# Scoring the far old keys of sample attention on VectorE, with later ScalarE parts and turns by chunk, in a one-core decoder step

## The chip, the core and the metric

The kernel runs on one core of a Trainium2 chip. The core has TensorE (PE; its weight loads are listed apart as PEld), VectorE (DVE), ScalarE (ACT), GpSimd (POOL) and SyncE (SP), which here issues nearly all DMA transfers. The metric is the device time of one execution in microseconds. The kernel before takes 2691.39 us, the median of three runs between 2690.68 and 2692.33.

## The reference

One layer of a decoder is computed for a prompt of 256 tokens and for 8 sequences of 8 new tokens each, which have 2048 cached keys and values. All is float32, and so are the weights. Cut to what matters here:

```python
x += 0.5 * swiglu(rmsnorm(x), w_ffa_in, w_ffa_out)
x += token_mixer(rmsnorm(x))
x += 0.5 * swiglu(rmsnorm(x), w_ffb_in, w_ffb_out)

# token_mixer
qk_pre, mv, mo, mif, aq, ak, av, gm, ga = split_cols(h @ w_in)
hm, state = mlstm(silu(conv(qk_pre)), mv, gates(mif), state)
hm = hm * rsqrt(mean(hm * hm) + EPS);  hm = sigmoid(mo) * hm * m_norm
ha = dilated_attention(aq * 128 ** -0.5, [cached k, ak], [cached v, av])
merged = sigmoid(gm) * (hm @ w_pm) + sigmoid(ga) * (ha @ w_pa)
return merged @ w_out

# mlstm, per head: the read-out
h = num / maximum(abs(den), exp(-m))

# dilated attention, 8 heads of 128 channels: three patterns (window, stride)
PATTERNS = ((128, 1), (512, 4), (2048, 16))
for (w, d), bias in zip(PATTERNS, biases):
    s = einsum('bthe,btjhe->bhtj', q, k_all[:, qi - d * arange(w // d + 1)]) + bias
    m = max(s); p = exp(s - m); den = sum(p); num = p @ v      # one part
# the parts are joined by their maxima and sums, as one softmax over all of them
```

For a sample token the first two patterns reach 512 positions back ("near" keys), the third up to 2048 at every 16th position. Of the old positions beyond 512 each of the 8 new tokens of a sequence has its own 96 ("far" keys): 16m + t for token t. So the 8 tokens together have 768 far keys, of which each uses every eighth.

## The kernel before, in words

**The stream of weights.** All weights are read from HBM once, in chunks of 512 KB (`raw`, five buffers, loaded by SP's queue): four blocks of 128 rows by 256 output columns. Every chunk is split into a high half (`hi`, a cast on ScalarE, L198) and a low half (`lo`, the difference on VectorE, L199), and the tokens likewise (`xh` and `xl`, `bh` and `bl`). The 320 tokens (256 of the prompt, 64 new ones) are the columns of each matmul. A chunk takes TensorE 24 matmuls into a foreground PSUM tile (`fg`): two column blocks, four row blocks, and three products xh·hi, xl·hi and xh·lo. `run_job` works off the chunks of one output tile; at each chunk it first runs the entries that `later` has put off, then splits the chunk two ahead (`split_upto(ci + HLB)`, three buffers of each half), then steps the background work, then issues the 24 matmuls, and then asks for the next loads. Each engine works in the order in which the program is written.

**The order of the jobs.** The first SwiGLU has chunks 0 to 271, the mixer's input projections 272 to 448 (attention's q, k and v first, then mLSTM's, then the gates gm and ga), `w_pm` 449 to 464 (eight jobs of two chunks), `w_pa` 465 to 480, `w_out` 32 chunks, then the second SwiGLU. `w_pm` multiplies the mLSTM heads' result (`hr`), `w_pa` the attention's (`ar`).

**Background work.** Prompt attention, sample attention and mLSTM are Python generators that wait in lists: `every` is stepped at each chunk, `even` and `odd` at every second one, and `slow`, which holds sample attention, at 8 of 15 chunks (`pace`). A step issues its instructions between the split and the chunk's matmuls, into background PSUM tiles (`bg`, four buffers). Whatever of it is left when the first job of `w_pa` opens is run off there by `pa_open`, and behind it come the four loads of `ar` and their split into `bh` and `bl`.

**Sample attention.** There are 16 units: two groups of four heads by eight sequences. A unit's scores are 128 rows (4 heads x a quarter of the keys x 8 tokens): 16 matmuls take 320 old keys each (`kd` against the queries `qbd`), of which 128 near and 192 far ones, and 4 small ones the new keys (`kS` against `qS`). A softmax over 328 columns follows (`ss`), three transposes turn the probabilities (`pts`), and 44 matmuls multiply them with the values (`vt`, `vn`). The result of a unit is scaled on its way out of PSUM into `osb`; after each fourth unit `combine` transposes four of them, copies them to `hsS`, and writes them to DRAM (`ha_d`), from which the split of `ar` reads.

Of the kernel before, what the change touches and what calls it, by code (L numbers as in the profile page):

```python
# [32 lines left out]
SCOLS = 328  # L33
# [23 lines left out]
def _consts():  # L57
# [4 lines left out]
    for i in range(4):  # L62
        for t in range(8):
            mk[:, i, t, 0:128] = _logmult(512 + t - 128 * i - p)
            mk[:, i, t, 128 + t:320:8] = 0.0
            if i == 0:
                mk[:, i, t, 320:328] = _logmult(t - np.arange(8))
# [19 lines left out]
    c["mix"] = np.concatenate([bd, sel, sels, parts, qmask, cm], axis=1)  # L87
# [9 lines left out]
M_BD, M_SEL, M_SELS, M_PT, M_QM, M_CM = 0, 32, 64, 128, 132, 388  # L97
MIXW = 836


def decoder_kernel(tc, I, O, K):
    nc = tc.nc
    V, S, G, T = nc.vector, nc.scalar, nc.gpsimd, nc.tensor
# [10 lines left out]

    def mm(out, a, b, start=True, stop=True, **kw):
        T.matmul(out, a, b, start=start, stop=stop, **kw)  # L116
# [11 lines left out]
    later_q = []  # L128
# [4 lines left out]
    def run_later(force=False):  # L133
        rest = []
        for e in later_q:
# [23 lines left out]
    RAWB, HLB, KDB = 5, 3, 6  # L159
# [84 lines left out]
    def run_job(job):  # L244
# [4 lines left out]
        for n, (ci, k0, nk) in enumerate(cs):  # L249
            run_later()  # L250
# [5 lines left out]
            if ci > 3:  # L256
                split_upto(ci + HLB)
            if tick[0] % 2 == 0:
# [52 lines left out]
    def tr(out, in_):  # L311
        k = in_.shape[0]
        T.transpose(out, in_, ident[:k, :k])  # L313
# [9 lines left out]
    vs_d = dp.tile([NS, 1024], F32, name="vs_d")  # L323
    qs_d = [dp.tile([128, 256], F32, name=f"qs_d{i}") for i in range(2)]
# [161 lines left out]
    def aq_evac(ps, p):  # L486
# [3 lines left out]
        QT[p] = q  # L490

# [96 lines left out]
    def sample_attention():  # L588
        bdm = M["mix"][:, M_BD:M_BD + 32]
        pts = mxt([128, 4, 152], "pts", 1, "pts")  # L590
        sm = mxt([128, 7, 32], "sm", 1, "sm")
        vn = mxt([128, 512], "vn", 1, "vn")
        G.memset(vn, 0.0)
        G.memset(pts, 0.0)
        G.memset(sm, 0.0)
        G.memset(sm[:, 4], 1.0)
        KD = {}

        def load_k(n):
            if n < 64:  # L600
                KD[n] = mxt([128, 4, 320], "kd", KDB, "kd")
                dma(KD[n], I["old_k"][n].rearrange("p (j c) -> p j c", j=4))

        VT = {}
# [24 lines left out]
        for n in range(KDB):  # L629
            load_k(n)  # L630
# [4 lines left out]
        for _ in range(3):  # L635
            yield
# [21 lines left out]

        def soft(u, sp):
# [3 lines left out]
            V.tensor_reduce(sm[:, 0, 0:1], s, op=OP.max, axis=AX.X)  # L663
# [4 lines left out]
            S.activation(s, s, AF.Exp, bias=sm[:, 3, 0:1], accum_out=sm[:, 4, 0:1])  # L668
            return s

        def keys(u, h):
            later(lambda: load_k(4 * u + KDB + h), 1)
# [6 lines left out]
        def pv(u, ob):  # L679
            cs = [(128, 0, 8 * i, i // 2, i % 2) for i in range(4)]  # L680
            cs += [(128, 1, 8 * i, 2 + i // 2, i % 2) for i in range(4)]
            cs += [(128, 2, 16 * i, 4, i) for i in range(2)]
            cs += [(128, 3, 0, 5, None)]
# [929 lines left out]
```

## Time and profile before

| | |
|---|---|
| time, median of 3 runs | 2691.39 us (2690.68 to 2692.33) |
| the profiled execution's own time | 2691.68 us |
| its span in the profile | 2689.9 us |
| mean granted TensorE clock | 0.998 of full speed |
| busy: PE, PEld | 99%, 98% |
| busy: DVE, ACT, POOL | 53%, 39%, 6% |
| DMA | 554.5 MB, 206 GB/s over the span |
| one chunk's matmuls on TensorE | 24 of 320 columns |

Busy shares are averages over the whole span. The first and the second SwiGLU are about two thirds of it and look alike throughout; attention and mLSTM lie between about 890 and 1660 us. There the lists of background work add matmuls to TensorE, small operations to VectorE and ScalarE, and the cached keys, values and states to the DMA queue. In the profile's rows an fp32 matmul leaves two records, so counts of them are twice those of the program. Durations of single matmuls overlap, since they are pipelined; the distance from start to start is what one costs.

### The profile page before, as it was taken

Reading aid. Unit: us, or ns where it says so; the run is one execution under the profiler, and the core shown is the slowest. Engines: PE = TensorE matmul, PEld = TensorE weight load, DVE = VectorE, ACT = ScalarE, POOL = GpSimd, SP = SyncE. Lnnn points to the kernel's source line nnn. Section 1 sums busy time; section 2 is a strip of 40 time slices with the busy share of each in tenths; the row PEclk is TensorE's granted clock in tenths of the full one; section 3 lists DMA queues with packets and bytes.
Section 4 is the critical chain, followed back from the end, with each engine's and each line's share of the span. In section 5 each row is a group of like instructions: output and inputs, shape, how many; then the busy total and the mean of one; then the engine's idle time right before and its main releaser. Section 6 shows DMA issues by size and latency. Waiting matters only on the chain.

```text
span 2689.9 us, 49844 instructions
## 1 busy us (share of the span) xinstructions
PE 2674.0 (99%) x21176; PEld 2635.3 (98%) x21176; DVE 1429.3 (53%) x1703; ACT 1051.0 (39%) x1289; POOL 156.7 (6%) x190
## 2 busy tenths in 40 slices
PE   9999999999999999999999999999999999999998
PEld 9999999999999999999999999999999999999998
DVE  6444444444446565666655555655444454444445
ACT  5333333333335433444443334444333333333334
POOL 0100000000000000111111100000000000000000
PEclk9999999999999999999999999999999999999999
DMA  6554545445546678798999986655454544445443
GB/s 236 164 164 165 159 163 164 158 160 162 165 157 199 227 257 287 272 366 314 344 349 330 330 285 218 204 184 163 157 165 161 161 164 161 161 153 171 163 152 131
DMA packets 186779, 554.51 MB, mean 206 GB/s; under 512 B 26288, under 2 KB 53432, under 8 KB 186556
## 3 DMA queue, kind: packets, MB, share of 16 engines
q1 hardware_dynamic: 185836, 550.02, 60.5%
q8 instruction: 165, 2.70, 0.4%
q10 hardware_dynamic: 720, 1.31, 0.1%
q14 instruction: 58, 0.48, 0.1%
HBM read 520.05 MB, written 31.20 MB: 205 GB/s over the span
## 4 chain that ended last, share of the span: by engine, by line
PE 98%; DVE 1%; DMA 1%; ACT 0%; issue 0%; SPq 0%; DVEq 0%; ACTq 0%
PE fg L116 92%; PE bg L116 5%; PE bg L313 1%; DMA raw<-in_w_ffa_in_dram 0%; DVE lo L199 0%; DMA x<-in_x_t_dram 0%; ACT hi L198 0%; DVE x L1506 0%; SPq L113 0%; DMA raw<-in_w_in_dram 0%; DVE ss L364 0%; DVE rows L783 0%; ACT sq L363 0%; DVE rows L792 0%; ACT lg L1494 0%
## 5 line engine op out<-in xcount | busy, mean ns | idle before, releaser
L199 DVE TENSOR_TENSOR lo<-raw,hi 128x1024 fp32r<-128x1024 f32 (+1 forms) x780 | 958.6, 1235 | 924.7 <-ACT hi L198 902.0
L116 PE MATMUL fg<-xh,hi 128*128 128x320 f32 x4232 | 1270.9, 301 | 1.5 <-ACT hi L1421 1.5
L116 PE MATMUL fg<-xh,lo 128*128 128x320 f32 x4232 | 1261.5, 299 | 0.5 <-DVE lo L199 0.5
L116 PE MATMUL fg<-xl,hi 128*128 128x320 f32 x4232 | 1261.3, 299 | 0.0
L198 ACT CAST hi<-raw 128x1024 fp32r<-128x1024 f32 (+1 forms) x780 | 797.2, 1027 | 1059.7 <-PE fg L116 926.0
L116 PEld LDWEIGHTS fg<-xh,hi 128*128 128x128 f32 x4232 | 798.5, 189 | 8.3 <-issue 4.9
L116 PEld LDWEIGHTS fg<-xh,lo 128*128 128x128 f32 x4232 | 798.6, 189 | 1.0 <-DVE lo L199 1.0
L116 PEld LDWEIGHTS fg<-xl,hi 128*128 128x128 f32 x4232 | 798.7, 189 | 0.7
L116 PE MATMUL fg<-hh,hi 128*128 128x320 f32 x1408 | 421.2, 299 | 0.0
L116 PE MATMUL fg<-hl,hi 128*128 128x320 f32 x1408 | 421.0, 299 | 0.0
L116 PE MATMUL fg<-hh,lo 128*128 128x320 f32 x1408 | 421.0, 299 | 0.0
L116 PEld LDWEIGHTS fg<-hh,hi 128*128 128x128 f32 x1408 | 266.1, 189 | 0.1
L116 PEld LDWEIGHTS fg<-hl,hi 128*128 128x128 f32 x1408 | 266.1, 189 | 0.1
L116 PEld LDWEIGHTS fg<-hh,lo 128*128 128x128 f32 x1408 | 266.1, 189 | 0.0
L424 POOL TENSOR_TENSOR gt<-gt,rstd 128x640 f32<-128x640 f32 x44 | 68.0, 1546 | 1775.6 <-ACT gt L423 1775.6
L116 PE MATMUL fg<-bh,hi 128*128 128x320 f32 x512 | 153.3, 299 | 0.0
L116 PE MATMUL fg<-bl,hi 128*128 128x320 f32 x512 | 153.1, 299 | 0.0
L116 PE MATMUL fg<-bh,lo 128*128 128x320 f32 x512 | 153.1, 299 | 0.0
L116 PEld LDWEIGHTS fg<-bh,hi 128*128 128x128 f32 x512 | 96.8, 189 | 0.2 <-issue 0.2
L116 PEld LDWEIGHTS fg<-bl,hi 128*128 128x128 f32 x512 | 96.8, 189 | 0.0
L116 PEld LDWEIGHTS fg<-bh,lo 128*128 128x128 f32 x512 | 96.8, 189 | 0.0
L412 ACT CAST hh<-hf 128x640 fp32r<-128x640 f32 x44 | 34.5, 785 | 144.3 <-DVE hf L430 144.3
(266 smaller groups left out, 1157.4 us busy)
## 6 DMA issues: line engine op xcount, KB each, us to landing
raw<-in_w_in_dram SPq DMA_DIRECT2D x176, 512.0 KB
raw<-in_w_ffb_in_dram SPq DMA_DIRECT2D x176, 512.0 KB
raw<-in_w_ffa_in_dram SPq DMA_DIRECT2D x172, 512.0 KB
raw<-in_w_ffa_out_dram SPq DMA_DIRECT2D x80, 512.0 KB
kd<-in_old_k_dram SPq DMA_DIRECT2D x64, 640.0 KB
vt<-in_old_v_dram SPq DMA_DIRECT2D x80, 512.0 KB
raw<-in_w_ffb_out_dram SPq DMA_DIRECT2D x80, 512.0 KB
raw<-in_w_out_dram SPq DMA_DIRECT2D x32, 512.0 KB
```

What stands on the lines that cost most here:

```text
L116: T.matmul(out, a, b, start=start, stop=stop, **kw)
L198: S.copy(hi[:, :nk], t[:, :nk])
L199: V.tensor_tensor(lo[:, :nk], t[:, :nk], hi[:, :nk].bitcast(F32), op=OP.subtract)
L313: T.transpose(out, in_, ident[:k, :k])
L412: S.copy(h, xe)
L424: G.tensor_tensor(gt, gt, bcast(rstd, 2), op=OP.mult)
```

## The change

**Far keys on VectorE.** The 16 score matmuls of a unit take 128 columns of near keys (`nk`) in place of 320. The far keys come as rows: `fk` tiles of 128 keys by four heads of 128 channels, six blocks a unit in three tiles. VectorE multiplies a block with the queries `qr` (the row of token t at each key of token t, read 16 times over from a copy of the queries in DRAM, `qt_d`, that each aq job now writes through two transposes). Four of the six blocks are summed by row on ScalarE (16 Copy activations with an accumulator, 128 x 128 each), two by a reduction on VectorE. The far keys have their own maximum, exponentials and sums: two numbers a head (`fr`) are brought into the near keys' score tile by four matmuls of two columns with a selection matrix `tsel`, and take part in its softmax as one more column. The far probabilities (`pf`) multiply the far values in 24 matmuls into columns of their own, and a `join` adds the two results with weights `rw`. The near probabilities need two transposes in place of three. Near keys come in 32 loads and far keys in 48, of 512 KB each; before there were 64 of 640 KB.

**Who is stepped when.** `pace` is gone. Sample attention is stepped with `even` at every second chunk, mLSTM stays on the other ones, and odd units have one step more. A new list, `fill`, holds the far keys' work; at each chunk it is stepped for as long as VectorE "has room": `Metered` counts 0.16 us and 0.00104 us an element for every VectorE instruction that goes through it, and compares with 3.2 us a chunk plus an allowance for the background matmuls.

**ScalarE's parts later.** A queue `soon` is run right behind the split, so that what is put there is issued behind the high half of the chunk that comes two later: the exponentials, the copies of the probabilities, the scaled copy and the join, the far row sums, and the mLSTM norm's logarithm and exponential.

**mLSTM's read-out.** |den| is taken by ScalarE. The heads are no longer divided by max(|den|, exp(-m)): its square, times EPS, is added under the root of the norm instead, which comes to the same result.

```diff
+class Metered:
+    def __init__(self, engine):
+        self.engine, self.load, self.debt = engine, 0.0, 0.0
+
+    def __getattr__(self, name):
+        fn = getattr(self.engine, name)
+
+        def call(*a, **k):
+            n = math.prod((a[1] if name == "tensor_reduce" else a[0]).shape[1:])
+            self.load += 0.16 + n * (0.0066 if name == "reciprocal" else 0.00104)
+            return fn(*a, **k)
+
+        return call
+
+    def next_chunk(self, tensor_us):
+        self.debt, self.load = max(0.0, self.debt + self.load - tensor_us), 0.0
+
+    def has_room(self, tensor_us):
+        return self.debt + self.load < tensor_us
...
+    def run_queue(q, force=False):
+        now, rest = q[:], []
+        q[:] = []
+        for e in now:
             e[0] -= 1
             if e[0] <= 0 or force:
                 e[1]()
             else:
                 rest.append(e)
-        later_q[:] = rest
-
-    every, even, odd, slow = [], [], [], []
-    pace = [0]
+        q[:0] = rest
...
+    every, even, odd, slow, fill = [], [], [], [], []
...
+            V.next_chunk(CHUNK_US + extra[0])
+            extra[0] = 0.0
...
             if ci > 3:
                 split_upto(ci + HLB)
+            run_queue(soon_q)
             if tick[0] % 2 == 0:
                 step(even)
+                step(slow)
             else:
                 step(odd)
             tick[0] += 1
-            pace[0] += 8
-            if pace[0] >= 15:
-                pace[0] -= 15
-                step(slow)
             step(every, now)
+            while fill and V.has_room(CHUNK_US + extra[0]):
+                if next(fill[0], True):
+                    break
...
+            tr(a[0:NS, m * 128:(m + 1) * 128], q[:, m, SEQ:NT])
+        s = m2_tile("qt")
+        S.copy(s[0:NS, 0:256], a[0:NS, 0:256])
+        later(lambda: dma(qt_d[:, p * 256:(p + 1) * 256], s[0:NS, 0:256]))
+        M["aq"] = p
...
+        def far_work():
+            for u in range(16):
+                while at["probs"] < u - 2 or u not in QR or tick[0] < since["q", u] + 6:
+                    yield True
+                SF[u] = sf = mxt([128, 6, 4], "fs", 2, "fs")
+                for n in range(3):
+                    i = 3 * u + n
+                    while i not in FK or tick[0] < since[i] + 5:
+                        yield True
...
+                    t = FK.pop(i)
+                    for a in range(2):
+                        V.tensor_tensor(t[:, a], t[:, a], QR[u], op=OP.mult)
+                        yield
+                        if n < 2:
+                            soon(lambda a=a, c=2 * n + a, t=t, sf=sf: far_rows(t[:, a], sf[:, c]), 2)
+                        else:
+                            V.tensor_reduce(sf[:, 4 + a], t[:, a].rearrange("p (h d) -> p h d", h=4), op=OP.add, axis=AX.X)
+                            yield
+                    later(lambda i=i: load_far(i + FKB), 4 if n < 2 else 1)
+                later(lambda u=u: load_qr(u + 2), 2)
+                yield True
+                yield True
+                V.tensor_tensor(sf, sf, M["fb"][:, u // 8], op=OP.add)
+                V.tensor_reduce(fm[:, 0, 0:4], sf.rearrange("p c h -> p h c"), op=OP.max, axis=AX.X)
...
+                soon(lambda sf=sf: S.activation(sf, sf, AF.Exp), 2)
+                yield True
+                yield True
+                yield True
+                while at["scores"] < u - 1:
+                    yield True
+                V.tensor_scalar(fr[:, :, 0], fm[:, 2, 0:4], lead, None, op0=OP.mult)
+                V.tensor_reduce(fr[:, :, 1], sf.rearrange("p c h -> p h c"), op=OP.add, axis=AX.X)
+                at["far"] = u
+                yield
+
+        def far_rows(t, out):
+            for h in range(4):
+                x = t[:, h * 128:(h + 1) * 128]
+                S.activation(x, x, AF.Copy, accum_out=out[:, h:h + 1])
+
+        def far_probs(u):
+            V.tensor_tensor(pf[:, 0:192].rearrange("p (a t) -> p a t", t=8),
+                            bcast(SF.pop(u).rearrange("p c h -> p (c h)"), 8, 2), bcast(tsel[:, 0:8], 24), op=OP.mult)
+            at["probs"] = u
...
-                    mm(sp[32 * h:32 * h + 32, 0:320], qbd[:, 4 * h + j], KD[4 * u + h][:, j], j == 0, j == 3,
+                    mm(sp[32 * h:32 * h + 32, 0:128], qbd[:, 4 * h + j], NK[2 * u + h // 2][:, h % 2, j], j == 0, j == 3,
                        tile_position=(0, 32 * h))
             for h in range(4):
                 c = (4 * hg + h) * 64 + 8 * b
-                mm(sp[32 * h:32 * h + 32, 320:328], M["qS"][:, c:c + 32], M["kS"][:, c:c + 8],
+                mm(sp[32 * h:32 * h + 32, 128:136], M["qS"][:, c:c + 32], M["kS"][:, c:c + 8],
                    tile_position=(0, 32 * h))
+            for h in range(4):
+                mm(sp[32 * h:32 * h + 32, 136:138], tsel, fr[:, h], tile_position=(0, 32 * h))
...
-            S.activation(s, s, AF.Exp, bias=sm[:, 3, 0:1], accum_out=sm[:, 4, 0:1])
+
+            def exps():
+                S.activation(s[:, 0:136], s[:, 0:136], AF.Exp, bias=sm[:, 3, 0:1], accum_out=sm[:, 4, 0:1])
+                S.activation(s[:, 136:137], s[:, 136:137], AF.Exp, bias=sm[:, 3, 0:1])
+
+            soon(exps)
...
+            for c in range(6):
+                v = VT[u, 2 + c // 2][:, c % 2]
+                for h in range(4):
+                    a = 8 * (4 * c + h)
+                    mm(ob[32 * h:32 * h + 32, 128:256], pf[:, a:a + 32],
+                       v[:, h * 128:(h + 1) * 128], c == 0, c == 5, tile_position=(0, 32 * h))
...
+                def join(u=u, ob=ob, o4=o4, o=o):
+                    V.scalar_tensor_tensor(o, ob[:, 128:256], rw[:, 1:2], o, op0=OP.mult, op1=OP.add)
+                    if u % 4 == 0:
+                        spawn(combine((u - 1) // 8, (u // 4 - 1) % 2, o4), even, True)
+
+                soon(lambda ob=ob, o=o: S.activation(o, ob[:, 0:128], AF.Copy, scale=rw[:, 0:1]))
+                soon(join, 2)
...
-            V.tensor_scalar(rd, B[:, 0:NT], -1.0, None, op0=OP.mult)
-            V.tensor_tensor(rd, rd, B[:, 0:NT], op=OP.max)
+            dq = mxt([128, NT], "dq", 1, "dq")
+            S.activation(rd, B[:, 0:NT], AF.Abs)
...
+            V.scalar_tensor_tensor(rs, ms[:, 0:NT], 1.0 / 256.0, d["dq"], op0=OP.mult, op1=OP.add)
+
+            def root():
+                if M["tanh"]:
+                    S.preload_act_table_set("natural_log_exp_and_others")
+                    M["tanh"] = False
+                S.activation(rs, rs, AF.Ln)
+                S.activation(rs, rs, AF.Exp, scale=-0.5)
+
+            soon(root)
...
-        while every or even or odd or slow:
-            run_later()
+        while every or even or odd or slow or fill or soon_q:
+            tick[0] += 1
+            run_both()
+            step(fill)
```

The first of three places in the order: TensorE's instructions of one unit in the middle of attention. `xl`/`xh` with `hi`/`lo` are a chunk's own matmuls; all others belong to the unit and to the one before it.

Before:

```order
L116 MATMUL fg<-xl,hi 128x320
L116 MATMUL fg<-xh,lo 128x320
L116 MATMUL bg<-vt,pts 32x128 x40
L116 MATMUL bg<-vn,pts 32x128 x4
L116 MATMUL bg<-kd,qbd 32x320 x16
L116 MATMUL bg<-kS,qS 32x8 x4
L116 MATMUL fg<-xh,hi 128x320
```

With the change:

```order
L145 MATMUL fg<-xh,lo 128x320
L145 MATMUL bg<-vt,pts 32x128 x16
L145 MATMUL bg<-vn,pts 32x128 x4
L145 MATMUL bg<-vt,pf 32x128 x24
L145 MATMUL bg<-nk,qbd 32x128 x16
L145 MATMUL bg<-kS,qS 32x8 x4
L145 MATMUL bg<-fr,mixc 32x2 x4
L145 MATMUL fg<-xh,hi 128x320
```

The 16 matmuls of 320 columns have become 16 of 128; the 40 with the old values are split into 16 and 24, and four of two columns are new.

The second place: SP's DMA issues round the last `combine`. `raw` are the weight chunks by matrix, `sg` the stored gates.

Before, among the jobs of `w_pm`:

```order
L113 DMA raw<-in_w_pm_dram 128x1024 x2
L113 DMA ha_d<-hsS 128x4x32
L113 DMA sg<-gate_d 128x640
L113 DMA raw<-in_w_pm_dram 128x1024
L113 DMA ar<-ha_d 128x2x320 x4
L113 DMA raw<-in_w_pm_dram 128x1024
L113 DMA sg<-gate_d 128x640
```

With the change:

```order
L137 DMA sg<-gate_d 128x640
L137 DMA raw<-in_w_pa_dram 128x1024 x2
L137 DMA ha_d<-hsS 128x4x32
L137 DMA ar<-ha_d 128x2x320 x4
L137 DMA sg<-gate_d 128x640
L137 DMA raw<-in_w_pa_dram 128x1024 x2
```

The write of the last quarter of the attention's result and the four loads that read it stood while `w_pm` chunks were still to be loaded; now they stand behind loads for `w_pa`. By chunks, the last `combine` was at 454 and is at 464, the last chunk ahead of `w_pa`.

The third place: ScalarE round the read-out of the last mLSTM head. `hi` are the high halves, `hh` the read-out, `re` its squares, `dq` the square of the denominator.

Before:

```order
L198 CAST hi<-raw 128x1024 x2
L1095 COPY hh<-bg 128x2x256
L1096 COPY hh<-bg 128x2x64
L198 CAST hi<-raw 128x1024 x2
L1106 ACTIVATE re<-hh 128x640
L198 CAST hi<-raw 128x1024 x2
```

With the change:

```order
L1243 COPY hh<-bg 128x2x256
L1244 COPY hh<-bg 128x2x64
L237 CAST hi<-raw 128x1024 x2
L745 ACTIVATE fk,fs<-fk 128x128 x16
L1252 ACTIVATE dq<-dq 128x320
L1253 ACTIVATE re<-hh 128x640
L237 CAST hi<-raw 128x1024 x2
```

Sixteen row sums of far keys (L745) stand between two high halves, the largest number that any chunk holds.

More of the change, by code (lines that the diff above doesn't have):

```diff
@@ L595, in sample_attention, with load_near, load_far, load_qr @@
         G.memset(sm, 0.0)
[L596 to L604, printed above, removed]
+        G.memset(sm[:, 4:6], 1.0)
+        G.memset(fm, 0.0)
+        G.memset(pf, 0.0)
+        NK, FK, QR, SF, VT, since = {}, {}, {}, {}, {}, {}
+        at = {"probs": -1, "scores": -1, "far": -1}
+        def load_near(n):
+            if n < 32:
+                NK[n] = mxt([128, 2, 4, 128], "nk4", NKB, "nk")
+                dma(NK[n], I["near_k"][n].rearrange("p (h j c) -> p h j c", h=2, j=4))
+        def load_far(n):
+            if n < 48:
+                FK[n] = mxt([128, 2, 512], "fk", FKB, "fk")
+                dma(FK[n], I["far_k"][n].rearrange("p (a c) -> p a c", a=2))
+                since[n] = tick[0]
+        def load_qr(u):
+            if u < 16:
+                hg, b = divmod(u, 8)
+                assert M["aq"] >= 2 * hg + 1
+                QR[u], since["q", u] = mxt([128, 512], "qr", 2, "qr"), tick[0]
+                dma(QR[u], raw_ap(qt_d[:], 8 * b * 1024 + hg * 512, [[1024, 8], [0, 16], [1, 512]]))
         def load_v(u, pc):
@@ new lines, in far_rows @@
+        def far_rows(t, out):
[6 more added lines that the diff above has]
+            at["probs"] = u
+        for n in range(NKB):
+            load_near(n)
+            yield
@@ L631, in sample_attention @@
+        for n in range(FKB):
+            load_far(n)
             yield
@@ L634, in sample_attention @@
         q4 = make_q4(0)
-        for _ in range(3):
-            yield
+        load_qr(0)
+        yield
+        load_qr(1)
+        fill.append(far_work())
         def make_qbd(u):
@@ L692, in probs, with copies @@
             tr(pt[:, 0:128], s[:, 0:128])
[L693 to L698 removed]
+            tr(pt[0:8, 128:256], s[:, 128:136])
+            def copies():
+                S.copy(pts[:, 0, 0:128], pt[:, 0:128])
+                S.copy(pts[0:8, 1, 0:128], pt[0:8, 128:256])
+            soon(copies)
             V.transpose(sm[:, 1], sm[:, 4])
             V.tensor_reduce(sm[:, 5, 0:8], sm[:, 1].rearrange("p (i t) -> p t i", i=4), op=OP.add, axis=AX.X)
[L701 removed]
             V.transpose(sm[:, 6], sm[:, 5])
+            V.scalar_tensor_tensor(rw[:, 0:1], s[:, 137:138], s[:, 136:137], sm[:, 6, 0:1], op0=OP.mult, op1=OP.add)
+            V.reciprocal(rw[:, 0:1], rw[:, 0:1])
+            V.tensor_tensor(rw[:, 1:2], rw[:, 0:1], s[:, 136:137], op=OP.mult)
+        yield
+        yield
         qbd = make_qbd(0)
@@ L711, in sample_attention @@
                 sp = scores(u, qbd)
+                at["scores"] = u
             if u:
@@ L721, in sample_attention @@
             values(u, 4, 0, 2)
-            keys(u, 0)
+            later(lambda u=u: load_near(2 * u + NKB), 1)
             yield
+            far_probs(u)
             if u < 15:
                 qbd = make_qbd(u + 1)
-            keys(u, 1)
+            later(lambda u=u: load_near(2 * u + 1 + NKB), 1)
             values(u, 1, 3, 5)
@@ L729, in sample_attention @@
             probs(s)
-            keys(u, 2)
             if u == 6:
@@ L733, in sample_attention @@
             yield
-            keys(u, 3)
-            yield
+            if u % 2:
+                yield
     def combine(hg, bg, o4):
```

125 lines of the change are left out of this document (69 added, 56 removed).

## The prediction

> **What bounds the kernel now.** I read the page's busy times and its chain of waits first, then the waits of each engine, then windows of the mixer, and last the timeline round the places that the change touches.
>
> ```profile
> span 2689.9 us, 49844 instructions
> PE 2674.0 (99%) x21176; PEld 2635.3 (98%) x21176; DVE 1429.3 (53%) x1703; ACT 1051.0 (39%) x1289; POOL 156.7 (6%) x190
> PE 98%; DVE 1%; DMA 1%; ACT 0%; issue 0%; SPq 0%; DVEq 0%; ACTq 0%
> ```
>
> The chain is TensorE from end to end. Its weight loads, which overlap the matmuls, are 98% busy as well, so there is next to no gap to close: time is won by taking matmuls away, and lost where TensorE is made to wait. ScalarE's and VectorE's splits wait for TensorE, not the other way round:
>
> ```profile
> ACT hi L198 <- PE fg L116: 926.0, 442, 3.4
> DVE lo L199 <- ACT hi L198: 902.0, 535, 4.8
> 1200.00:1300.00 100.00, 100.00 (x1024) 92.52 (x1024) 64.68 (x117) 42.34 (x67) 16.59 (x29) 1.00 0.93 338
> 1400.00:1500.00 100.00, 100.00 (x1014) 92.97 (x1015) 55.74 (x85) 34.49 (x51) 14.06 (x22) 1.00 0.95 348
> ```
>
> (The windows' columns are PE, PEld, DVE, ACT, POOL, clock, DMA share, GB/s.) In the mixer VectorE is 56 to 65% busy, ScalarE 34 to 42%.
>
> **What TensorE is spared.** One unit of sample attention in the timeline, start to start, since a matmul's own duration holds its pipeline:
>
> ```profile
> 1289.61 2.39 PE L116 MATMUL bg<-vt,pts 128*32 128x128 f32 x80
> 1291.82 0.40 PE L116 MATMUL bg<-vn,pts 128*32 128x128 f32 x8
> 1292.03 2.34 PE L116 MATMUL bg<-kd,qbd 128*32 128x320 f32 x32
> 1294.19 0.22 PE L116 MATMUL bg<-kS,qS 128*32 128x8 f32 x8
> 1294.34 0.40 PE L116 MATMUL fg<-xh,hi 128*128 128x320 f32 x1
> ```
>
> Each fp32 matmul leaves two records. The old keys' scores take 2.16 us for 32 records of 320 columns; 128 columns cost 2.21/80 = 0.0276 us a record. With 128 columns the same 32 records take 0.88, so a unit saves 1.28 and 16 units **20.4 us**. The values stay at 44 matmuls of 128 columns (40 + 4 before, 16 + 4 + 24 now): no change. The four new two-column matmuls with `tsel` are taken like the four of 8 columns, 0.15 us: 16 x 0.15 = **+2.4** (from 8 records at the floor of nothing, 0, to 8 records of 128 columns, 3.5).
>
> ```profile
> 1308.69 0.60 PE L313 MATMUL bg<-ident,osb 128*128 128x128 f32 x4
> 1309.12 0.49 PE L313 MATMUL bg<-ident,ss 128*128 128x128 f32 x3
> 1309.37 0.38 PE L116 MATMUL fg<-xh,hi 128*128 128x320 f32 x1
> 1309.59 0.30 PE L116 MATMUL fg<-xl,hi 128*128 128x320 f32 x1
> 33.22 846.78 PE fg L116 x6234
> ```
>
> Four transposes take 1309.12 - 1308.69 = 0.43, 0.11 each. A unit has one fewer for its probabilities: **-1.7** in 16 units. The eight new ones for the queries cost **+0.9**. After a background group the second projection matmul comes 0.22 behind the first (1309.37 to 1309.59) instead of 846.78/6234 = 0.136; the order has about ten more such groups, since attention and mLSTM no longer share chunks: **+0.9**. Sum on TensorE: -20.4 - 1.7 + 2.4 + 0.9 + 0.9 = **-17.9 us**.
>
> **What VectorE and ScalarE take on.** Rows that price it:
>
> ```profile
> L116 PE MATMUL bg<-kd,qbd x512: 432/432/457, 972.7 to 1579.7; 128*32 128x320 f32 x171
> L199 DVE TENSOR_TENSOR lo<-raw,hi 128x1024 fp32r<-128x1024 f32 x748 | 936.7, 1259 | 918.1 <-ACT hi L198 895.4 <-PE bg L116 4.0 <-DMA raw<-in_w_in_dram 3.6
> L858 DVE TENSOR_TENSOR pre<-fg,rstd 128x512 f32<-128x512 f32 x8 | 5.5, 690 | 7.0 <-PE fg L116 5.7 <-DMA vm_d<-stage 1.2
> L198 ACT CAST hi<-raw 128x1024 fp32r<-128x1024 f32 x748 | 778.8, 1044 | 1051.0 <-PE fg L116 917.3 <-issue 62.8 <-ACT hi L198 49.3
> 938.24 0.40 ACT L546 ACTIVATE s<-s,ns 128x128 f32<-128x128 f32 x1 [2.55 <-DVE ns L545]
> 938.55 0.18 ACT L546 ACTIVATION_READ_ACCUMULATOR s<-s,ns 128x1 f32 x1
> 938.64 0.49 ACT L547 ACTIVATE s<-s,ns 128x256 f32<-128x256 f32 x1
> ```
>
> The scores' first and last start give attention's stretch: 607 us for 15 units, some 640 with the last. VectorE: six products and two reductions of 512 elements a unit, 8 x 0.69 = 5.5, and about a dozen small operations, say 0.2 each: +8 a unit at most, 127 in all, 20% of the stretch: 64% becomes 84% or less, since narrower scores and copies leave it. ScalarE: 16 row sums a unit. One with its accumulator read holds the engine 938.64 - 938.24 = 0.40 us, 6.4 a unit, 102 in all, 16%: 42% becomes 58%. On average both lie beside TensorE and cost **nothing**; without that cover it would be up to 229 us.
>
> Nothing, too, for the rest. The mLSTM denominators go from VectorE to ScalarE and lose a reciprocal, four times in all, off the path. The score exponentials, the copies of the probabilities and the join of the two value sums come a chunk or two later than before, behind the next high half; by the order TensorE asks for them two chunks after that at the earliest, 6.5 us, against 0.4 to 0.6 us of work. Old keys come as 32 + 48 loads of 512 KB in place of 64 of 640 KB, the same bytes, issued where the old ones were; the queries' way through DRAM adds four small writes and 16 reads. On SP's queue the weight loads behind them are asked for five chunks before their split, so a hold of one chunk there reaches nobody.
>
> What would cost is a late split. A projection chunk is 24 x 0.136 = 3.26 us. Its halves are split two chunks ahead: high half at the start of a chunk (1.04), low half behind it (1.26), wanted two chunks or 6.5 us later, so 4.2 us of backlog are covered. By the order most chunks hold 8 row sums (3.2 us, covered); two hold 16: 1.04 + 6.4 + about 1 of other work, 5.2 over the chunk, some 0.6 to 1 more than the cover. I take **+1.2** for both and the four chunks with 12 (0 if other chunks give slack, 11 if the read of the accumulator adds its 0.18 to each).
>
> **What waits at the end of attention.** Here lies the one new wait that I am sure of. The last `combine` moves from the third `w_pm` job to the last chunk before `w_pa`. There its result goes to DRAM, comes back as `ar` and is split before the first `w_pa` matmul, and TensorE has only that one chunk in hand. Before, ten chunks lay between:
>
> ```profile
> 1622.49 1.05 ACT L198 CAST hi<-raw 128x1024 fp32r<-128x1024 f32 x1 [2.21 <-PE fg L116]
> 1624.71 0.28 DVE L744 COPY hsS<-bg 128x128 f32<-128x128 f32 x1
> 1625.24 0.39 SPq L113 DMA_DIRECT2D ha_d<-hsS  x1
> 1628.90 1.97 SPq L113 DMA_DIRECT2D ar<-ha_d  x4
> 1632.17 0.49 SPq L113 DMA_DIRECT2D sg<-gate_d  x1
> 1639.65 0.74 ACT L1295 ACTIVATE sg<-sg 128x640 f32<-128x640 f32 x1 [2.64 <-DMA sg<-gate_d]
> 977.83 0.24 SPq L113 DMA_DIRECT2D sT_d<-sT  x1
> 979.77 0.34 SPq L113 DMA_DIRECT2D sTb<-sT_d  x1
> L412 ACT CAST bh<-ar x4: 805/806/806, 1656.5 to 1658.6; 128x640 fp32r<-128x640 f32 x4
> L413 DVE TENSOR_TENSOR bl<-ar,bh x4: 819/822/825, 1657.7 to 1660.0; 128x640 fp32r<-128x640 f32 x4
> ```
>
> Count from the chunk's start, here 1622.5. The copy is issued behind the low half and its write follows at +2.75. A write and the dependent read behind it stand 1.94 apart in the small pair at 977.83, at most 3.66 here: `ar` goes out at +4.7 to +6.4, I take +5.0. Six loads of 2.16 MB, the four `ar` among them, had landed 10.75 us after the first issue (1639.65); less 1.94 that is 1.3 us for each 320 KB, so the first `ar` lands at +8.3, the second at +9.6. With 0.81 for the high and 0.82 for the low half these are ready at +9.95 and +11.2. TensorE is done at 0.43 + 3.26 = +3.7 and can put six matmuls (0.8) between the two: it stands 11.2 - 3.7 - 0.8 = 6.7 us by this count, 8.5 with the later read. I take **+7.3** (0 below, if the transfers are hidden; 8.5 above).
>
> Who stands behind that wait: on ScalarE, behind the four casts of `ar`, a sigmoid and the high half of the third `w_pa` chunk; on VectorE the four low halves, the last `w_pm` product and that chunk's low half. The fourth cast ends about +13, the low half some 3.5 later, near +16.5; TensorE, starting at +10, wants it two chunks on, +17 or later. So nothing further is late. On SP the four `ar` now stand behind seven `w_pa` loads instead of among `w_pm` loads; those were issued a chunk or more before, and the next load behind `ar` is split only five chunks later.
>
> Idling also costs clock:
>
> ```profile
> 2676.00:2680.00 4.00, 1.89 (x9) 1.06 (x8) 0.49 (x1) 1.99 (x5) 0.00 (x0) 1.00 0.00 0
> 2680.00:2689.00 9.00, 0.00 (x0) 0.00 (x0) 4.61 (x8) 0.40 (x2) 3.03 (x2) 0.52 0.78 291
> 0.99 4.10 PE L116 MATMUL bg<-ones 128*128 128x128 f32 x20 [0.99 <-POOL epst L399]
> L313 PE MATMUL bg<-ident,ss x48: 271/273/329, 989.5 to 1593.5; 128*128 128x128 f32 x32, 128*72 128x128 f32 x16
> ```
>
> Within two us of TensorE's last matmul the granted clock is at half (0.52), and the first 20 fp32 records of the program take about 3.9 us start to start where later ones would take 20 x 0.11 = 2.2. I add **+1.7** (0 if the clock holds, 3.4 for a double dose). The Trainium skill, "TensorE: Matmul & The Clock Gate", Part 1, says the clock halves after an idle window of about 3.4 us and needs a busy one to return; by it the wait would cost an estimated 1.7 to 3.4, and the rows agree.
>
> **Sum.** The profiled execution took 2691.7 (span 2689.9 and 1.8 around it), 0.3 over the median of the runs, 2691.4. 2691.4 - 17.9 + 7.3 + 1.7 + 1.2 = **2683.7**, say 2684, 0.27% less.
>
> **Rivals.** *The last wait is hidden* (7%): 2684 - 9 = 2675. For it speaks only that transfers may be quicker than the rows; against, that TensorE has no other work queued there.
>
> *ScalarE's row sums decide* (20%): each costs 0.58 because the read does not overlap; a chunk of 16 then stalls TensorE some 3.5, one of 12 about 1: 2684 - 1.2 + 11 = 2694. The 938.64 row speaks against it, the bunching in the order for it.
>
> *VectorE is held* (11%), the one that ends slower. VectorE is in order: a product waits for its keys' DMA, the score sum for ScalarE's row sums, and the next low half stands behind it. Up to 4.2 us a hold is free; beyond, TensorE pays. At 6 us in each unit that is 16 x 1.8 = 29: 2713; it undoes the gain from about 4.7. Against it: keys are asked for five chunks (over 16 us) ahead and sums are taken at least three chunks behind the products. For it: DMA is 0.93 to 0.95 busy there, and the queries' copies add 16 x 256 KB.
>
> ```profile
> 1280.00:1290.00 10.00, 10.00 (x89) 9.83 (x91) 6.23 (x9) 3.00 (x4) 0.75 (x2) 1.00 1.04 411
> ```
>
> The mean of 348 GB/s has room: ten us ran at 411, and the copies ask for about 8 GB/s. The Trainium skill, "DMA: Bandwidth & Descriptors", section "Where 436 GB/s comes from", holds HBM loads to about 358 GB/s a core; by that this stretch would be full and this rival likelier. The 411 row disagrees, so I leave it at 11%.
>
> **Chances.** The forecast has 62% (2679 to 2690, a quarter of it above 2686). Less than 0.2% (5.4 us) can't be told from no change. Faster: 0.47 + 0.07 = 0.54; same: 0.15 + 0.19 = 0.34; slower 0.12. Eight in ten: 2677 to 2694, from the hidden wait to ScalarE's row sums.
>
> **What would show it.** Right: `nk,qbd` near 0.9 us a unit, one PE gap of 6 to 9 us ended by `bl<-ar` with a clock dip behind it, no other wait of PE above 1 us. Wrong: PE waits on `lo` or `fr` inside the mixer, or no gap before `w_pa`.

## The result, and the profile after

The changed kernel takes 2707.53 us (median of four runs, 2704.78 to 2713.37), the kernel before 2691.6 beside it: a ratio of 1.0062, with an interval of 1.0045 to 1.008. It is slower, by 16 us. The forecast was 2684, with 2677 to 2694 as its range: wrong in sign.

The page of the changed kernel, for the lines that opened the prediction, and the waits of TensorE (us in total, times, longest):

```profile
span 2705.9 us, 50989 instructions
PE 2669.5 (99%) x21296; PEld 2644.2 (98%) x21296; DVE 1515.7 (56%) x1995; ACT 1126.1 (42%) x1847; POOL 159.4 (6%) x192
PE 91%; DMA 5%; DVE 2%; ACT 1%; issue 1%; SPq 0%; DVEq 0%; ACTq 0%
...
PE bg L145 <- DMA vn<-vs_d: 5.5, 2, 3.2
PE fg L145 <- ACT bh L456: 4.2, 1, 4.2
PE bg L145 <- DMA C<-in_state_C_dram: 3.0, 1, 3.0
PE bg L145 <- issue: 2.3, 1, 2.3
PE fg L145 <- DVE lo L114: 1.8, 2, 1.3
```

TensorE is still "99% busy", since a matmul's own duration hides short gaps, but the chain of waits now has 5% of DMA in it. `vn` are the new values of a unit (16 KB), `C` the mLSTM states of two sequences (256 KB each). Windows of ten us round the five largest waits, with the columns PE, PEld, DVE, ACT, POOL, clock, DMA share, GB/s:

```profile
1165.00:1175.00 10.00, 7.47 (x47) 6.20 (x47) 9.72 (x31) 4.59 (x10) 1.17 (x2) 0.81 0.99 328
1323.00:1333.00 10.00, 7.04 (x41) 5.35 (x40) 4.96 (x9) 2.67 (x5) 0.00 (x0) 0.83 1.04 397
1378.00:1388.00 10.00, 7.72 (x154) 7.27 (x153) 3.99 (x14) 3.39 (x17) 0.73 (x1) 0.83 1.04 394
1457.00:1467.00 10.00, 6.79 (x127) 6.38 (x129) 1.23 (x1) 4.98 (x20) 0.00 (x0) 0.72 1.04 403
1664.00:1674.00 10.00, 5.62 (x33) 5.03 (x32) 3.08 (x4) 2.81 (x4) 0.00 (x0) 0.78 0.82 262
```

In each the granted clock is below full speed. In the first VectorE is busy 97% of the time. In the middle three the DMA engines are busy all the time; the last is the wait ahead of `w_pa`, where they are not.

**An account of TensorE.** To compare kernels I split the time from the first matmul to the last in three, by start-to-start distances in the trace: what a matmul usually takes before its successor at full clock (the median of that pair of instructions), what goes beyond it by over 0.25 us (a wait), and what goes beyond it while the clock is at half. Waits under 0.25 us stay in the first part, so it is good to some 3 us, and the parts of a single wait are less sure than the sums.

| profiled run | matmuls alone | waits | half clock |
|---|---|---|---|
| before | 2674.1 | 3.4 | 0 |
| the change | 2653.3 | 26.4 | 13.4 |

The change does spare TensorE 20.8 us, and loses 23.0 us in waits and 13.4 in half clock. Of these 7.0 us (5.3 and 1.7) belong to the wait ahead of `w_pa`. The other 29 lie in the mixer between 940 and 1470 us, at seven places, where the prediction had 1.2.

### The profile page after: what moved, and what is told of

It is laid out like the page before. It is cut to its first block, busy times and chain, and to the rows that moved or that the text cites. A ratio compares the mean times of both kernels' runs of the same rounds, so it can differ in the third digit from the quotient of the medians.

```text
span 2705.9 us, 50989 instructions
## 1 busy us (share of the span) xinstructions
PE 2669.5 (99%) x21296; PEld 2644.2 (98%) x21296; DVE 1515.7 (56%) x1995; ACT 1126.1 (42%) x1847; POOL 159.4 (6%) x192
## 4 chain that ended last, share of the span: by engine, by line
PE 91%; DMA 5%; DVE 2%; ACT 1%; issue 1%; SPq 0%; DVEq 0%; ACTq 0%
PE fg L145 87%; PE bg L145 3%; DMA raw<-in_w_in_dram 2%; DMA vt<-in_old_v_dram 1%; ACT hi L237 1%; DMA vn<-vs_d 1%; DVE lo L114 1%; PE bg L356 0%; DMA qr<-qt_d 0%; SPq L137 0%; DMA re<-rows_d 0%; DVE fk L114 0%; DMA out_C_sample_dram<-C 0%; ACT fk L745 0%; DVE x L114 0%
```

## The experiments

Times are medians; "before" beside them took 2691.1 to 2691.9. Ratios are to before, with their intervals.

### The rhythm

My first theory was that of late loads. In even units `vn` is now asked for three chunks ahead of its use, where it was four and a half (three steps of two chunks less three chunks put off; before, four steps of 15/8). In the changed kernel's timeline (start, duration, and in brackets the wait) the load that ends a wait was issued 7.0 us before it is used, and had not landed:

```profile
1455.52 0.30 SPq L137 DMA_DIRECT2D vn<-vs_d  x1
1458.22 1.08 PE L145 MATMUL bg<-vt,pts 128*32 128x128 f32 x32
1462.51 0.66 PE L145 MATMUL bg<-vn,pts 128*32 128x128 f32 x8 [3.21 <-DMA vn<-vs_d]
```

**The old rhythm in the changed kernel.**

```diff
-                step(slow)                # with even
+            pace[0] += 8
+            if pace[0] >= 15:
+                pace[0] -= 15
+                step(slow)
...
-            if u % 2:
-                yield
+            yield
```

> The changed kernel with the old rhythm of sample attention: stepped at 8 of 15 chunks, five steps in every unit. Theory, late loads: TensorE waits in the mixer because the last load of a unit's values (vn) is asked for three chunks ahead of its use in even units, where it was four and a half before, and takes 7 to 8 us to land in full DMA queues; here the distance is the old one, the two waits for vn and the half clock behind them (12.6 us) go, the waits for C stay, and the wait ahead of w_pa grows by 3 to 5 us, since the last combine moves one chunk on: 2699 us. Rival, VectorE is held by the far keys whatever the rhythm: the waits stay or change their name, 2707 us or more.

2694.36 us, 1.0011 (1.0001 to 1.002): 13 us less than the change. Waits for `vn` are still there (two, 7.1 us, at other units), so the way I expected it is not the whole way.

**The new rhythm in the kernel before** (`step(slow)` with `even`, four steps and in odd units five).

> The kernel before, with the new rhythm alone: sample attention stepped at every second chunk, mLSTM on the others, four steps in even units and five in odd ones. It computes all that the kernel before does. Theory, late loads: vn is asked for three chunks ahead in even units here too, so waits for it of 2 to 3 us with the clock behind them appear in some of the eight even units: 2697 to 2705 us. Rival, the far keys' work is what holds the loads up: 2690 to 2693 us, no wait for vn above 1 us.

2695.70 us, 1.0018 (1.0009 to 1.0027): 4.6 us more than before. In its trace (of the slowest of ten runs, 2699.98 us) the largest wait is a new one at the first unit, for the queries `qbd`; for values and `vn` only one unit waits:

```profile
PE bg L116 <- POOL qbd L637: 3.2, 1, 3.2
PE bg L116 <- DMA vt<-in_old_v_dram: 1.3, 1, 1.3
PE bg L116 <- DMA vn<-vs_d: 1.1, 1, 1.1
```

So the rhythm alone is not what loses 29 us. In the changed kernel the old rhythm gives 13 back, but with it the far keys' results (`fr`) also come earlier ahead of the scores that need them, 12.7 us in the mean against 9.8, and these two runs do not tell the one from the other.

### Asking earlier

**`vn` one chunk behind the last reader of its buffer.**

```diff
             values(u, 4, 0, 2)
+            later(lambda u=u: load_v(u, 5), 1)
...
-            values(u, 1, 3, 5)
+            values(u, 1, 3)
```

> The changed kernel, with vn asked for four chunks earlier, one chunk behind the last reader of its buffer. Theory, late loads: the waits at 1380 and 1459 us go with their clock, 5.9 + 6.8 us, and nothing else moves: 2695 us. Rival, VectorE is held and vn is only the last of several late inputs: 2705 to 2708 us.

2701.6 us, 1.0034 (1.0024 to 1.0043): half of what was expected. In its trace (of the fastest of ten runs, 2695.18 us) the waits for `vn` are gone; the one for `C` is there and longer (4.3 us in place of 3.0).

**`C` one mLSTM step earlier** (`load_cc` ahead of the `yield` in place of behind it).

> The changed kernel, with the mLSTM states C of the sequences after next asked for one mLSTM step (two chunks, 6.5 us) earlier. Theory, late loads: the waits for C at 1169 and 1325 us and what follows from them, some 7 us and 3 us of clock, go: 2697 us; the first of them belongs to a pair that is asked for elsewhere and may stay: then 2701. Rival: 2705 to 2708 us.

2708.14 us, 1.0061 (1.0046 to 1.0076): nothing. No wait is put down to `C` any more; those for `vn` are three, of 6.5 us, in place of two, of 5.5.

**Both.**

> The changed kernel, with both vn and C asked for earlier. Theory, late loads: 2701.6 with vn alone, whose trace still waits 5.7 us for C with 1.9 us of clock behind it; these go too: 2694 us. Rival, with one late load mended the next one takes its place: 2700 us or more.

2701.83 us, 1.0037 (1.0022 to 1.0051): the rival's number. With both loads early, low halves are late six times:

```profile
PE fg L145 <- DVE lo L114: 4.6, 6, 2.1
```

ScalarE waits longer for weight chunks too. What it waits for ahead of a high half, in the kernel before, in the change and in this one:

```profile
ACT hi L198 <- DMA raw<-in_w_in_dram: 6.3, 2, 3.2
```

```profile
ACT hi L237 <- DMA raw<-in_w_in_dram: 20.2, 8, 6.0
```

```profile
ACT hi L237 <- DMA raw<-in_w_in_dram: 42.9, 13, 6.8
```

Mending one request moves the lateness to another: it is not one request that is late. But ScalarE's wait for weight chunks does not measure what TensorE loses. In the fastest kernel (allowance 4.2 and `vn` early, below), where TensorE waits for no low half longer than 0.5 us, it is

```profile
ACT hi L237 <- DMA raw<-in_w_in_dram: 33.0, 10, 7.0
```

### The other edits of the change

**The last combine four chunks ahead of `w_pa`** (`if u % 2 and u < 12`).

> The changed kernel, without the extra step of the last two odd units: the last combine moves from the last chunk ahead of w_pa to four chunks before it. Theory: the wait ahead of w_pa (5.3 us in the changed kernel's trace) and the half clock behind it (1.7) go, all else stays: 2700.5 us. Rival, the time is given back elsewhere (another wait ahead of w_pa, or the shorter units wait for vn): 2705 us or more.

2701.99 us, 1.004 (1.0025 to 1.0055): 5.5 us less, where the trace had 7.0. The wait is gone from the trace; it was real, as forecast.

**The root of the norm issued at once** (`root()` for `soon(root)`).

> The changed kernel, with the logarithm and the exponential of the mLSTM norm issued at once again, not behind the next high half. Theory: they (and their table load of 1.3 us) no longer stand ahead of the copies that ks needs, so the wait for nP and ks at 1274 us goes, with its clock 3.2 us, perhaps the 1.5 us at 1158 as well: 2703 to 2705 us. Rival, ScalarE's later parts cost TensorE nothing: 2706 to 2709 us.

2708.87 us, 1.0067 (1.0052 to 1.0082): nothing. The wait at 1274 us goes, and longer ones stand elsewhere (3.5 us for `vn` at 1287). ScalarE's later parts were tried in this one place only.

### Less for the DMA queues

**29 of the 32 near-key loads left out.**

```diff
+                if n >= NKB:
+                    NK[n] = NK[n % NKB]
+                    return
```

> The changed kernel, with 29 of the 32 loads of near keys left out (the first three tiles are used over and over, so the sample tokens' attention is not the reference's): 15 MB less in the mixer, all instructions of the engines as they were. Theory, full DMA queues make the loads late: a small load lands in 3 us instead of 7 to 8, the waits for vn and C go with their clock (12.6 and about 10 us): 2685 to 2690 us. Rival, SP issues them late or VectorE is held, and the queues' load is not the matter: 2703 to 2708 us.

2694.48 us, 1.0013 (1.0004 to 1.0023). **14 of the 16 copies of the queries left out**, in the same way:

> The changed kernel, with 14 of the 16 copies of the queries (256 KB each, every row read 16 times over) left out: the first two are used over and over, so the sample tokens' attention is not the reference's. 3.7 MB less in the mixer. Theory, bytes in full queues: 15.2 MB of near keys were worth 13 us, so 3 us: 2704 us. Rival, the copies cost the queues more than their bytes: 2700 us or less. Rival, they cost nothing: 2706 to 2709 us.

2697.27 us, 1.0023 (1.0014 to 1.0032). Both help, by 13 and 10 us, so the fullness of the queues has a part in it. But by bytes (15.2 and 3.7 MB) the second should have been worth 3; the copies also hold SP longer than a load of 512 KB, as its rows in the changed kernel have it:

```profile
1442.35 0.62 SPq L137 DMA_DIRECT2D qr<-qt_d  x1
...
1446.70 0.33 SPq L137 DMA_DIRECT2D raw<-in_w_in_dram  x1
```

Which of the two counts was not separated.

### The allowance of VectorE

Two versions were built to be faster. **Units spread by DMA load**: ten to twelve chunks a unit among the states, eight elsewhere; `vn` early; and `CHUNK_US`, the number that `has_room` compares with, raised so that the far keys keep up:

```diff
-    CHUNK_US = 3.2
+    CHUNK_US = 4.2
...
-            if u % 2:
+            for _ in range((4 <= u < 11) + (u in (5, 6, 8, 9))):
```

> The changed kernel with attention's units spread by DMA load: eight chunks a unit ahead of and behind the stretch in which mLSTM's states are read and written, ten to twelve within it; vn asked for earlier; VectorE's allowance a chunk raised from 3.2 to 4.2 us, so that the far keys do not lag; the last combine four chunks ahead of w_pa. Theory, DMA queues are full where units of eight chunks meet the states: the waits for vn, C and values go, the wait ahead of w_pa too; left are some 5 us at 1042 (a late low half) and 1158 to 1170 us: 2680 to 2685 us, faster than the kernel before. Rival, far keys hold VectorE: with the larger allowance more low halves are late, 2695 us or more.

2679.92 us, 0.9957 (0.9944 to 0.9971). **The old rhythm with a faster end**, `vn` early, allowance 3.6:

> The changed kernel with the old rhythm (8 of 15 chunks, five steps a unit) up to the twelfth unit, four steps from then on, vn asked for earlier, allowance 3.6 us, the last combine eight chunks ahead of w_pa. Theory: 2694.4 of the old rhythm, less its wait ahead of w_pa with the clock (8 us), less its waits for vn (8.6 us and up to 6 of clock, half of which a later load takes up): 2680 us. Rival: other waits take their place, 2690 us or more.

2689.12 us, 0.9992 (0.9983 to 1.0001), 9 us more than expected; two waits for old values (`vt`), 7.1 us, are new. The first seemed to bear out full queues. **Its allowance alone** shows that it does not:

> The changed kernel with one number of the fastest version alone: VectorE's allowance a chunk 4.2 us instead of 3.2. Far keys no longer lag (the pause of 14 chunks between two units goes), and the last combine comes at chunk 454, eleven ahead of w_pa. Units of eight and ten chunks still meet the mLSTM's states, and vn is asked for as late as in the change. Theory, full DMA queues and late requests: only the wait ahead of w_pa goes, 7 us, the waits for vn and C stay: 2698 to 2703 us. Rival, far keys that lag and then bunch are what makes the loads late: they go too, 2688 us or less.

2678.05 us, 0.995 (0.9937 to 0.9964), 29.5 us less than the change, by one number. One wait for `vn` is left in its mixer (2.8 us). The queues are no less full. Three windows of 100 us, of the change and then of this version:

```profile
1100.00:1200.00 100.00, 96.13 (x907) 92.97 (x906) 72.31 (x151) 51.30 (x135) 15.72 (x31) 0.97 0.85 299
1200.00:1300.00 100.00, 98.58 (x1051) 94.41 (x1050) 78.44 (x162) 53.38 (x154) 17.73 (x31) 0.98 0.83 291
1300.00:1400.00 100.00, 94.76 (x891) 90.07 (x890) 70.92 (x145) 52.85 (x150) 15.46 (x26) 0.97 0.96 350
```

```profile
1100.00:1200.00 100.00, 99.76 (x962) 96.75 (x962) 82.20 (x181) 58.63 (x174) 19.26 (x34) 1.00 0.97 356
1200.00:1300.00 100.00, 100.00 (x1071) 96.59 (x1070) 80.37 (x178) 55.84 (x146) 18.25 (x32) 1.00 0.91 330
1300.00:1400.00 100.00, 96.77 (x925) 91.95 (x925) 74.11 (x154) 53.59 (x163) 12.27 (x25) 0.98 0.99 371
```

What differs is when the far keys are done. In the change VectorE has only 72% of its time filled between 1100 and 1200 us and the queues 0.85; here 82% and 0.97. The far keys' result of a unit (`fr`) and the scores that need it, at the eighth unit, in the change and in this version:

```profile
1288.01 0.19 DVE L114 TENSOR_REDUCE fr<-fs 128x4 f32<-128x24 f32 x1
1291.28 1.05 PE L145 MATMUL bg<-nk,qbd 128*32 128x128 f32 x32
```

```profile
1218.70 0.19 DVE L114 TENSOR_REDUCE fr<-fs 128x4 f32<-128x24 f32 x1
1246.95 1.06 PE L145 MATMUL bg<-nk,qbd 128*32 128x128 f32 x32
```

3.3 us ahead against 28.3. Over 16 units the mean is 9.8 against 22.9, and in the change four units get it with 0.6 to 3.3 us to spare. TensorE waits for no `fr` there, since the meter counts while the program is built and the holds stand in the order itself. The far keys lag, and attention is held for them: its units start at chunks 308, 316, 326, 334, 344, then 358, 368, 376, then 388; with the allowance 306, 314, 324, 332, 342, 350, 360, 368, 378.

**The same positions without the lag.** Attention held by hand to the change's chunks, allowance 4.2:

```diff
+            for _ in range({0: 3, 5: 3, 8: 1}.get(u, 0)):
+                yield
             while at["far"] < min(u, 15):
```

> The changed kernel with the allowance of 4.2 us, and its units of attention held by hand to the very chunks they have in the change (308, 316, 326, 334, 344, 358 and so on to 450, last combine 464). Theory, positions: what makes loads and halves late is where units meet mLSTM's and prompt attention's work; the waits come back, 2700 to 2709 us. Rival, the far keys' lag itself: their products are done earlier here than in the change, at the same positions of all TensorE work; only the wait ahead of w_pa (7 us) comes back, 2685 us.

2688.83 us, 0.9994 (0.9985 to 1.0002). TensorE's work stands at the chunks that it has in the change, and the time is 18.7 us less. Of the 10.8 us that it is over the allowance alone, its trace has 7.8 ahead of `w_pa` (5.2 of wait, 2.6 of clock). So positions are worth some 3 us, and the lag, the later time at which the far keys' work is done, 18.7.

**An allowance between** (3.6 us):

> The changed kernel with the allowance at 3.6 us, between the change's 3.2 and the 4.2 of the faster version. Attention starts at chunk 308 as in the change, but the pause of 14 chunks at its sixth unit is gone and one pause of two chunks is left; last combine at 458, so the wait ahead of w_pa is gone. Theory, the far keys' lag makes loads late: much of the lag is gone, 2678 to 2686 us. Rival, 3.2 and 4.2 differ by chance collisions: anything from 2680 to 2700, with waits for vn and C as in the change.

2684.21 us, 0.9974 (0.9964 to 0.9985): between, as the lead of `fr` is (14.0 us in the mean). **No limit** (99 us):

> The changed kernel with the allowance set so high that VectorE's load never holds the far keys back; only their loads and the order of their steps do. Theory, the count of VectorE's time is not needed, only its holding back costs: 2676 to 2681 us, as with 4.2. Rival, VectorE is held by bunches of products, low halves come late: 2685 us or more.

2692.57 us, 1.0007 (0.9998 to 1.0016): here the rival is right. What TensorE waits for with no limit:

```profile
PE fg L145 <- DVE lo L114: 3.5, 5, 1.4
PE bg L356 <- DVE C L114: 2.9, 2, 2.5
PE bg L145 <- DVE z L114: 1.7, 1, 1.7
```

All VectorE's own work, late because far-key work stands ahead of it. The units stand at the chunks that they have with 4.2, so here too only the far keys' time differs. And `fr` leads by 29.6 us in the mean, more than anywhere else: a long lead alone does not make the kernel fast. The four values, 3.2, 3.6, 4.2 and no limit, give 2707.5, 2684.2, 2678.1 and 2692.6.

**Allowance 4.2 and `vn` early:**

> The changed kernel with the allowance of 4.2 us and vn asked for earlier. The version with the allowance alone took 2678.05; its trace has one wait left in the mixer, for vn at 1321 us, 3.0 us with 2.4 of half clock behind it. Theory, a late request: it goes, 2673 us. Rival, another load takes its place: 2677 to 2680 us.

2676.84 us, 0.9946 (0.9934 to 0.9959), the fastest, though not to be told from the allowance alone (2678.05). The account of TensorE for these kernels, each from one profiled run (that of `vn` early was 6.4 us below its median, the others within 3 us of theirs):

| profiled run | matmuls alone | waits | half clock |
|---|---|---|---|
| the change | 2653.3 | 26.4 | 13.4 |
| old rhythm | 2654.5 | 20.3 | 7.7 |
| `vn` early | 2656.3 | 19.4 | 5.1 |
| allowance 4.2, held | 2655.4 | 13.0 | 6.7 |
| no limit | 2655.7 | 16.6 | 3.3 |
| allowance 4.2 | 2653.1 | 6.5 | 2.4 |
| allowance 4.2, `vn` early | 2656.2 | 4.2 | 0 |

The matmuls alone take the same in all. The kernels differ in waits and in the clock behind them.

## Why the prediction was wrong

**What TensorE is spared: right.** -17.9 us forecast, -20.8 measured. A unit's scores in the changed kernel:

```profile
1144.33 1.06 PE L145 MATMUL bg<-nk,qbd 128*32 128x128 f32 x32
1145.20 0.22 PE L145 MATMUL bg<-kS,qS 128*32 128x8 f32 x8
1145.27 0.22 PE L145 MATMUL bg<-fr,mixc 128*32 128x2 f32 x8
```

0.87 us start to start, where 0.88 was forecast.

**The wait ahead of `w_pa`: right in place, a little large.** 7.3 and 1.7 of clock forecast; 5.3 and 1.7 in the trace, and 5.5 for both when taken away. (The upper bound of 8.5 is 8.1 by the prediction's own steps: a read 1.4 later than +5.0.) The step that was too long was the read behind the write, forecast at +5.0 and issued at +3.2. ScalarE's and SP's rows there:

```profile
1663.60 1.04 ACT L237 CAST hi<-raw 128x1024 fp32r<-128x1024 f32 x1 [2.21 <-PE fg L145]
1666.31 0.43 SPq L137 DMA_DIRECT2D ha_d<-hsS  x1
1666.79 4.06 SPq L137 DMA_DIRECT2D ar<-ha_d  x4
1670.74 1.62 ACT L456 CAST bh<-ar 128x640 fp32r<-128x640 f32 x2 [6.09 <-DMA ar<-ha_d]
```

From the chunk's high half the first `ar` is there at +7.1, not +8.3, though its issue follows the write's by 0.5 us.

**"On average both lie beside TensorE and cost nothing": the step that failed.** As an average it held: VectorE is 71% busy between 1000 and 1600 us, below the 84% allowed for. But the far keys do not take VectorE's free time; they take what `has_room` lets them have. I read `Metered` as a guard against late halves, and did not ask whether its allowance suffices, nor whether its prices are right. Some are high: mLSTM's convolution on VectorE, in the changed kernel's timeline, takes 0.31 us an instruction where the meter counts 0.16 + 256 x 0.00104 = 0.43.

```profile
1164.00 1.85 DVE L114 SCALAR_TENSOR_TENSOR y<-pre,gv,y 128x256 f32<-128x256 f32 x6
```

This step cost 18.7 us at the same positions of TensorE's work, and 29.5 with the positions and the wait ahead of `w_pa` that follow from it. The order had the pauses in it (14 chunks between the fifth and the sixth unit) and I listed unit positions without asking what held them. The rival that VectorE decides was in the list, at 2713 and 11%, but the other way round: as too many products ahead of a low half. That one exists too, with no limit at all, and at one place of the change (below); here the far keys were in the main too late.

**"Wanted five chunks later, so a hold of one chunk there reaches nobody": wrong in what it covered.** It holds for weight chunks that are asked for in time. `vn` and `C` stand in the same queues. In the three waits put down to them, TensorE wants them 3.6 to 6.0 us after their issue and has them after 7.0 to 8.5. In the changed kernel weight chunks too keep ScalarE waiting eight times, for 20.2 us; as the fastest kernel shows, that need not reach TensorE.

**The clock: a right price, put on one wait.** Five places in the mixer cost half clock as well, some 11 us there in all.

**ScalarE's row sums (1.2 us, and a rival of 2694).** At one place of the change they and VectorE's products do what the two rivals said, on a small scale. At 1043.5 us TensorE waits 1.3 us for a low half that VectorE made behind a far-key sum and a product. Then sixteen row sums stand between two high halves; from the first to the last of them:

```profile
1039.56 1.03 ACT L237 CAST hi<-raw 128x1024 fp32r<-128x1024 f32 x1
1040.49 0.30 ACT L745 ACTIVATE fk<-fk 128x128 f32<-128x128 f32 x1
...
1044.89 0.29 ACT L745 ACTIVATE fk<-fk 128x128 f32<-128x128 f32 x1
1046.01 1.03 ACT L237 CAST hi<-raw 128x1024 fp32r<-128x1024 f32 x1
```

They hold ScalarE for 4.7 us, 0.29 each where 0.40 was priced, and TensorE waits 0.7 us twice, at 1047.5 and 1049.1, for work that stands behind them. So the term was about as large as forecast there. With the allowance at 4.2, with as many row sums, there is no wait at this place, and 6.5 us in the whole run.

**What stays open.** That the lag costs 18.7 us is shown by the held version; by which way is not. Late loads are a part of it: with the lag TensorE waits 8.5 us for `vn` and `C`, at the same positions without it 4.3. It may be that products done late free their buffers late, so that the queues run at 0.83 to 0.85 from 1100 to 1300 us and lack that time afterwards; the two runs with less to load speak for it, since their far keys lag as in the change (`fr` leads by 9.3 and 9.4 us). But the held version has queues as full, 0.99 from 1300 to 1400 us, and one wait there. It may be that VectorE's halves are later: of the 165 chunks from 300 to 464, the low half ended less than 2 us ahead of its first matmul in 2 before, in 15 with the change, in 3 with the allowance; but in 11 in the held version. More buffers for the far keys, which would part the two, were not tried.

## What to carry to other kernels

A limit that meters background work on an engine with time to spare is itself a resource: if it grants less than the work needs, the work lags, what needs its results is held for it, and other inputs come late, with no engine but the one that bounds the kernel near 100% on average. Sweep such a limit to both sides before judging the change that brought it; here one number decided between 16 us slower and nearly 14 us faster. And count not only an engine's mean load but the margin with which its results arrive: the time from `fr` to its scores showed the lag, which busy shares did not. It shows a lag and no more: with no limit the margin was the largest, and the kernel slower again.

## What the runs showed of the hardware

A wait of 1.4 us could be enough to lose the clock, for a fixed time after it. In the changed kernel's timeline, and in a window behind it (the column after POOL is the clock):

```profile
1275.55 0.50 PE L145 MATMUL bg<-vs,ks 32*128 32x256 f32 x4 [1.42 <-DVE nP L114]
```

```profile
1277.00:1279.00 2.00, 2.00 (x10) 2.00 (x9) 1.90 (x6) 0.57 (x4) 0.49 (x2) 0.51 1.02 259
```

The clock is at half from 1277.0 to 1280.4. Windows of two us round the wait for `vn` that ends at 1462.5 in the changed kernel:

```profile
1458.00:1460.00 2.00, 1.30 (x35) 0.86 (x33) 0.25 (x1) 1.94 (x5) 0.00 (x0) 1.00 1.07 398
1460.00:1462.00 2.00, 0.00 (x0) 0.00 (x0) 0.98 (x1) 2.00 (x15) 0.00 (x0) 0.84 1.05 421
1462.00:1464.00 2.00, 1.49 (x29) 1.52 (x33) 0.00 (x0) 0.07 (x1) 0.00 (x0) 0.50 1.03 403
1466.00:1468.00 2.00, 2.00 (x46) 1.98 (x39) 0.30 (x1) 0.00 (x0) 0.00 (x0) 0.50 1.03 403
1468.00:1470.00 2.00, 2.00 (x16) 2.00 (x16) 1.81 (x7) 0.00 (x0) 0.00 (x0) 0.96 1.03 419
```

This wait of 3.4 us has 6.8 us at half clock, of which 5.7 lie behind it; TensorE loses half of these, 2.8, in addition. In all traces the stretches at half clock behind such waits last 3.4 or 6.8 us. The Trainium skill, "TensorE: Matmul & The Clock Gate", Part 1, has windows of about 3.4 us that run freely, which these lengths agree with; it names a whole idle window as the condition, where the waits of 1.4 us at 1274 and of 2.5 us at 1380 each brought 3.4 us at half clock. With both loads early, a wait of 2.7 us at 1458 cost none: by these runs the length alone does not decide.

The DMA queues ran at 371 GB/s over 100 us (1300 to 1400, allowance 4.2), beside one wait of 2.8 us in TensorE. The Trainium skill's "DMA: Bandwidth & Descriptors", section "Where 436 GB/s comes from", holds a core's loads from HBM to about 358 GB/s, half of what two cores share. One core ran here, and the row counts writes as well, so it does not contradict it, but a stretch at that rate need not stand still.
